# Hybrid decoder trunk on one Trainium2 core: order of the second layer's gates and retention outputs

## The chip, the core and the metric

The kernel runs on one core of one Trainium2 chip. The core has a matrix engine (PE, TensorE) that multiplies from SBUF into the eight banks of PSUM, a vector engine (DVE), an activation engine (ACT), GpSimd (POOL) and a queue (SP) that issues most transfers. Each engine works through its own list of instructions in order, and the lists are tied by semaphores. The metric is the time of one execution on the device in microseconds, lower is better.

## The reference

Two layers of a decoder trunk, over 512 tokens of width 1024, in f32. Of each layer:

```python
h = rmsnorm(x, g_mix)
z = h @ w_in
aq, ak, av, rq, rk, rv, rg, ga, gb = jnp.split(z, SPLIT_POINTS, axis=-1)
...
ya = sliding_window_sink_attention(aq, ak, av, sinks) @ w_a
...
r = chunkwise_retention(rq, rk, rv)
r = r * lax.rsqrt(jnp.mean(r * r, axis=-1, keepdims=True) + EPS)
r = r.reshape(B, S, RET_V) * jax.nn.silu(rg.astype(jnp.float32))
yb = r.astype(x.dtype) @ w_b
mixed = jax.nn.sigmoid(ga) * ya + jax.nn.sigmoid(gb) * yb
x = x + mixed @ w_out
h2 = rmsnorm(x, g_mlp)
x = x + jnp.square(jax.nn.relu(h2 @ w_up)) @ w_down
```

Retention has four heads, with 128 query and key columns and 256 value columns each. The change concerns the stretch from the values `rv` to the product with `w_b`: four heads of retention, their norm over 256 columns, the gated inputs `rg` (eight blocks of 128 columns, two for each head), and the gates `gb` (eight blocks).

## The kernel before

**Precision and tiles.** Activations are held transposed: 128 columns of the model on the partitions, 512 tokens along a row. Every operand of a large product is split into a high and a low part (`split`: ACT copies the high part as `r` or `hi`, DVE subtracts to get the low part as `r` or `lo`, L364/L365, L311/L312), and a product is three matmuls, high by high, high by low and low by high (`products`, L357 to L359). Weights come in units of 128x1024 (512 KB), loaded by SP into three `raw` buffers, split into three pairs of `hi` and `lo`, three units ahead of use. The list `unit_order` says in which order; it has to be the order of use.

**A chunk** (`chunk`) is one weight unit against all 512 tokens: 24 matmuls into one PSUM bank of `ps_mm` (five banks), after which a function evicts the bank. The chunks of `w_in` that matter here:

- `qk(h)`: k, then q of retention head h. `put_ret` rotates (`rotate`: two temps, `rot` and `rot2`, ACT L736/L737, DVE L740 to L742) and splits.
- `put_rg(i)`, i = 0..7: gated input i, scaled by the row norm into half of a `big` tile `z` (L1097), then Silu (L1104) for i >= 4 at once.
- `put_aside(c)`, c = 0..7: gate c into half of a `big` tile `gb` (L966), Sigmoid (L967), and for every second one a store to DRAM (`aside`), from which it is read back before its use.

**Values in the second layer** (`all_values`): seven block products (a Strassen-Winograd form, with the sums of the input made ahead), two weight units each, into `rv` banks. The first four value blocks `rv[0, n]` (heads 0 and 1) are complete after the fifth product, `rv[1, 2]` and `rv[1, 3]` (heads 2 and 3) after the sixth, `rv[1, 0]` and `rv[1, 1]` after the seventh. The bank pair `b` is read by DVE (`kept`, L1057) between the sixth and the seventh.

**Retention as a background.** `all_heads` is a generator whose steps are put between the parts of the chunks: each call `advance(rate)` adds the rate to a credit and takes one step for each whole unit of it. A chunk calls it twice, before each half of its matmuls; `all_values` 14 times with 0.6. A step emits instructions, so it sets the place of the work in the source. A head's steps: `scores` (two steps; products `ret`, tiles `s`, four in all), `outputs` (two steps; PSUM tiles `r` and `last` of `ps_aux`, three banks; `big` tile `rr`, temps `sq` and `rest`), `norm` (PSUM tile `ssq`, then square root and reciprocal into the temp `inv`), `finish` (products with `inv` and with `rr`, L1194/L1195, and a split for each half). After two heads `sum_heads` makes the sums that the block form of W_b needs (`sums`, L667 to L671, two `big` tiles), and splits them.

Three norms exist: `inverse_rms` (one square root and one reciprocal over 128x512), `inverse_rms_apart` (four square roots on 32 rows each, a reciprocal of 128x128, and a round trip through DRAM by two SP transfers, `row` and `inv`, L482/L483), and `inverse_rms_halved` (two square roots and a reciprocal over 256 columns, four copies back, L493 to L497). Heads 0 to 2 use the one that goes apart, head 3 `inverse_rms`. The MLP norm uses the halved one.

**Buffers.** `temp` tiles share one tag of six buffers of 128x512; `big` tiles one tag of seven of 128x1024.

**After the gates**: `drain` takes all steps that are left, then the first two pairs of W_b products (`mixed_pair`, `narrow_pair`: seven groups of 12 matmuls of 256 columns, the first pair in the three banks of `ps_aux`) read the splits of heads and sums.

**Order.** Engines don't follow the source strictly: the framework places each instruction on its engine's list by a simulation of the program, earlier source first among what is ready. What it has placed is fixed, and the chip then works through it.

The diff's places: `unit_order` (second layer's list), `Head.norm`, `Head.finish`, `all_heads`, and the calls at the end of the mix in `layer_body`. `Head` serves both layers, the rest of the edits the second alone.

Of the kernel before, what the change touches and what calls it, by code (L numbers as in the profile page):

```python
# [14 lines left out]
ALU = mybir.AluOpType  # L15
# [3 lines left out]
P = 128  # L19
T = 512  # L20
# [3 lines left out]
NB = T // P  # L24
# [5 lines left out]
RET_V = 256  # L30
# [29 lines left out]
def unit_order(last):  # L60

    def plain(name, *at):
        return [(name, i) for i in range(*at)]

    def pairs(src, *firsts):
        return [("pair", j, part, src) for j in firsts for part in range(4)]

    if last:
        order = plain("w_in", 22) + plain("w_a", 4)
        order += [("value", block, u) for block in range(len(VALUES)) for u in range(2)]  # L70
        order += plain("w_in", 26, 30) + plain("w_in", 34, 46)
    else:
        order = plain("w_in", 26) + plain("w_a", 4) + plain("w_in", 26, 46)
    order += pairs("w_b", 0, 2) + plain("w_b", 4, 8)
    order += plain("w_out", 2) + pairs("w_out", 2, 4, 6)
    for what, q, i in mlp_sequence():
        if what == "first":
            order += plain("w_up", 4)
        elif what == "pair":
            order += pairs("w_up", 8 * q + 2 * i)  # L80
        elif what == "down":
            order += plain("w_down", 8 * q + 2 * i, 8 * q + 2 * i + 2)
        else:
            order += plain("w_down", 8 * q, 8 * q + 8)
    return order


def mlp_sequence():

    seq = [("first", 0, 0), ("pair", 0, 2), ("pair", 0, 3)]
    for q in range(3):
        for i in range(4):
            seq += [("down", q, i), ("pair", q + 1, i)]
    return seq + [("last", 3, 0)]
# [32 lines left out]
def view(slot):  # L129
    return slot[0][:, slot[1], :]  # L130
# [3 lines left out]
def decoder(ctx, tc, xT, x_first, w_in, w_a, w_b, w_out, w_up, w_down, tables, decay, band, triangles, g_last, out):  # L134
    nc = tc.nc
# [10 lines left out]
    def f32(ap):  # L146
        return ap.bitcast(F32)
# [7 lines left out]
    def bank(pool, name):  # L155
        return pool.tile([P, T], F32, tag=pool.name, name=name)
# [15 lines left out]
    order = [(layer, *u) for layer in range(DEPTH) for u in unit_order(layer == DEPTH - 1)]  # L172
# [144 lines left out]
    def unit(name, layer):  # L317
        i = state["next"]
        assert order[i][:2] == (layer, name), (order[i], layer, name)
        state["next"] += 1  # L320
        split_until(i + 3)
        return parts.pop(i)
# [28 lines left out]
    def products(ps, pairs, start, stop, resume=False):  # L351


        n = len(pairs)
        for i, ((ah, al), (bh, bl)) in enumerate(pairs):
            more = {"skip_group_check": True} if resume else {}
            nc.tensor.matmul(ps, ah, bh, start=start and i == 0, stop=False, **more)  # L357
            nc.tensor.matmul(ps, ah, bl, start=False, stop=False, **more)  # L358
            nc.tensor.matmul(ps, al, bh, start=False, stop=stop and i == n - 1, **more)  # L359

    def split(hi, lo, src, scale=None):

        if scale is None:
            nc.scalar.activation(hi, src, AF.Copy)  # L364
            nc.vector.tensor_tensor(lo, src, f32(hi), ALU.subtract)  # L365
        else:
            nc.scalar.activation(hi, src, AF.Copy, scale=scale)
            nc.vector.scalar_tensor_tensor(lo, src, scale, f32(hi), ALU.mult, ALU.subtract)

    xs, x_homes = [], []  # L370
# [13 lines left out]
    def advance(rate=1.0):  # L384

        credit[0] += rate
        while credit[0] >= 1.0:
            credit[0] -= 1.0
            while background:
                try:  # L390
                    next(background[0])
                    break
                except StopIteration:
                    background.pop(0)
# [5 lines left out]
    def chunk(name, layer, moving, evacuate, rate=1.0):  # L400

        hi, lo = unit(name, layer)
        n = len(moving)
        ps = bank(ps_mm, "mm")
        pairs = [((hi[:, k * P : (k + 1) * P], lo[:, k * P : (k + 1) * P]), moving[k]) for k in range(n)]
        advance(rate)
        products(ps, pairs[: n // 2], True, False)
        advance(rate)
        products(ps, pairs[n // 2 :], False, True)
        evacuate(ps)  # L410
# [232 lines left out]
    def layer_body(layer):  # L643
        last_layer = layer == DEPTH - 1
# [351 lines left out]
        def qk(h, rate=1.0, between=lambda: None):  # L996
            chunk("w_in", layer, xs, put_ret(rk, h), rate)
            between()
            chunk("w_in", layer, xs, put_ret(rq, h), rate)

        rv = {}
# [86 lines left out]
        rg, rg_next, rg_tiles = {}, {}, {}  # L1088

        def put_rg(i):  # L1090
            def put(ps):
                if i % 2 == 0:
                    two = rg_tiles[i // 2] = big("z")
                    rg[i], rg_next[i + 1] = two[:, 0, :], two[:, 1, :]
                else:
                    rg[i] = rg_next.pop(i)
                nc.vector.tensor_tensor(rg[i], ps, rstd(), ALU.mult)  # L1097
                if i >= 4:
                    silu(i)

            return put
# [12 lines left out]
        class Head:  # L1114
# [70 lines left out]

            def norm(self):
                self.inv = temp("inv")
                (inverse_rms if self.h == 3 else inverse_rms_apart)(self.parts, RET_V, self.inv)

            def finish(self):  # L1190
                h = self.h
                for e in range(2):
                    z = rg.pop(2 * h + e)
                    nc.vector.tensor_tensor(z, z, self.inv, ALU.mult)  # L1194
                    nc.vector.tensor_tensor(z, self.rr[e], z, ALU.mult)  # L1195
                    hi, lo = slots.one(), slots.one()
                    split(view(hi), view(lo), z)
                    ret[2 * h + e] = (hi, lo)

        def retention(pair):  # L1200
# [34 lines left out]
        def all_heads():  # L1235
            four = [Head(h) for h in range(RET_HEADS)]

            def scores(h):
                while h not in rq:
                    yield  # L1240
                for js in ((0, 1), (2, 3)):
                    four[h].scores(js)
                    yield

            def outputs(h, *es):
                for e in es:
                    four[h].outputs(e)
                    yield

            yield from scores(0)  # L1250
            yield from scores(1)
            while (0, NB - 1) not in rv:
                yield
            yield from outputs(0, 0, 1)
            yield from outputs(1, 0)
            yield
            four[0].norm()
            yield
            yield from outputs(1, 1)
            yield from scores(2)  # L1260
            four[1].norm()
            yield
            yield from scores(3)
            for head in four[:2]:
                head.finish()
                yield
            sum_heads(0)
            yield
            yield from outputs(2, 0, 1)
            yield from outputs(3, 0)  # L1270
            four[2].norm()
            yield
            yield from outputs(3, 1)
            yield
            yield
            four[3].norm()
            yield
            for head in four[2:]:
                while 2 * head.h + 1 not in rg:
                    yield  # L1280
                head.finish()
                yield
            sum_heads(1)
# [27 lines left out]
        for u in range(4):  # L1311
            hi, lo = unit("w_a", layer)
            for j in range(2):
                c = 2 * u + j
# [15 lines left out]
        if last_layer:  # L1330
            background.append(all_heads())
            all_values(form_of(by_form_v), homes_v)
            qk(2, 1.1)
            qk(3, 1.1)
        else:
            background.append(retention(0))
            qk(2)
            qk(3)
            values(1)
            drain()  # L1340
            background.append(retention(1))
        for i in range(4, 8):
            chunk("w_in", layer, xs, put_rg(i), 1.1 if last_layer else 1.25)
        gates, gate_tiles, fresh = [], [], []

        def put_aside(c):
            def put(ps):
                if c % 2 == 0:
                    fresh[:] = [big("gb")]
                gate(fresh[0][:, c % 2, :])(ps)  # L1350
                if c % 2:
                    nc.sync.dma_start(aside[:, c - 1 : c + 1, :], fresh[0])

            return put

        for c in range(KD):
            chunk("w_in", layer, xs, put_aside(c), 1.1 if last_layer else 1.25)
        drain()
        old_input()

# [472 lines left out]
```

## Time and profile before

| | us |
|---|---|
| median of 3 runs | 1478.62 |
| lowest and highest | 1478.37, 1480.4 |
| profiled execution | 1478.1 |
| its span, first to last instruction | 1476.3 |

Times below are from the span's start. The second layer's values run to about 942, its qk chunks, gated inputs and gates from there to 1044.8, the W_b pairs from 1044.8. In the rows of the timeline stand the start, the duration, engine, line, operation, the tile written and the tiles read; in brackets the idle time of the engine before it and what ended it. In the list of waits stand the waiter, what it waited for, the total in us, how often and the longest. In the windows stand, for each engine, the busy time with the number of instructions, then the granted clock of PE (1.00 is full), the share of DMA and its rate. Matmul durations overlap, so their spacing is what counts.

### The profile page before, as it was taken

The numbers are of one execution on the slowest core, as the hardware profiler recorded it, in microseconds if no ns is written. First come the engines' busy times: TensorE is split into PE (matmuls) and PEld (weight loads), VectorE is DVE, ScalarE is ACT, GpSimd is POOL, SyncE is SP. The second block draws the span as 40 slices with busy tenths as digits, with TensorE's granted clock in tenths as the row PEclk, the third lists the DMA queues.
The fourth block names the chain that finished last, engine by engine and source line by source line (L and its number), as shares of the span: only waits on it lengthen the run. The fifth ranks groups of instructions, "written<-read, shape, count | busy, mean of one in ns | idle before, by whom it ended". The sixth has DMA issues, their size and how long they took to land.

```text
span 1476.3 us, 20312 instructions
## 1 busy us (share of the span) xinstructions
PE 1461.0 (99%) x7410; PEld 1245.2 (84%) x7410; DVE 1187.1 (80%) x1950; ACT 830.9 (56%) x1330; POOL 3.7 (0%) x14
## 2 busy tenths in 40 slices
PE   9999999999999999999999999999899999999998
PEld 7888888888988888888888888788789888888887
DVE  7998778678988787776898888677899877877774
ACT  7657356654784444544465675556547754455544
POOL 0000000000000000000000000000000000000000
PEclk9999999999999999999999999999899999999999
DMA  6423843356443333235963237633464432333363
GB/s 226 132 89 105 278 161 106 94 179 209 129 130 105 100 115 105 95 100 168 340 237 111 86 129 227 233 104 118 142 204 122 138 104 88 120 109 100 111 193 110
DMA packets 80548, 212.30 MB, mean 144 GB/s; under 512 B 9512, under 2 KB 9664, under 8 KB 80448
## 3 DMA queue, kind: packets, MB, share of 16 engines
q1 hardware_dynamic: 80160, 210.48, 44.5%
q8 instruction: 58, 0.95, 0.3%
q10 hardware_dynamic: 288, 0.52, 0.1%
q14 instruction: 42, 0.34, 0.1%
HBM read 183.16 MB, written 25.18 MB: 141 GB/s over the span
## 4 chain that ended last, share of the span: by engine, by line
PE 95%; DVE 2%; DMA 1%; issue 1%; ACT 0%; SPq 0%; POOLq 0%; DVEq 0%; ACTq 0%
PE mm L359 23%; PE mm L357 23%; PE mm L358 23%; PE mm L1517 11%; PE mm L1518 6%; PE rv L357 1%; PE rv L358 1%; PE rv L359 1%; PE score L905 1%; DMA park_w_out<-ahead 1%; DVE lo L312 1%; PE r L357 1%; PE r L359 0%; PE r L358 0%; PE pT L860 0%
## 5 line engine op out<-in xcount | busy, mean ns | idle before, releaser
L358 PE MATMUL mm<-r,hi 128*128 128x512 f32 (+1 forms) x1568 | 574.1, 368 | 2.6 <-DVE r L365 2.6
L357 PE MATMUL mm<-r,hi 128*128 128x512 f32 (+1 forms) x1568 | 571.0, 368 | 3.1 <-ACT r L364 2.8
L359 PE MATMUL mm<-r,lo 128*128 128x512 f32 (+1 forms) x1568 | 564.9, 368 | 0.3 <-DVE lo L312 0.2
L311 ACT ACTIVATE hi<-raw 128x1024 fp32r<-128x1024 f32 (+1 forms) x340 | 340.1, 1003 | 370.2 <-PE mm L358 200.6
L312 DVE TENSOR_TENSOR lo<-raw,hi 128x512 fp32r<-128x512 f32 (+1 forms) x341 | 391.7, 1151 | 106.5 <-ACT hi L311 105.2
L357 PEld LDWEIGHTS mm<-r,hi 128*128 128x128 f32 x1568 | 295.5, 189 | 50.7 <-ACT r L364 3.2
L358 PEld LDWEIGHTS mm<-r,hi 128*128 128x128 f32 x1568 | 295.9, 189 | 49.4 <-DVE r L365 3.2
L359 PEld LDWEIGHTS mm<-r,lo 128*128 128x128 f32 x1568 | 295.0, 189 | 48.8 <-DVE lo L312 1.5
L1517 PE MATMUL mm<-r,hi 128*128 128x512 f32 x728 | 251.9, 391 | 0.0
L1518 PE MATMUL mm<-r,lo 128*128 128x256 f32 x728 | 200.3, 277 | 0.0
L1517 PEld LDWEIGHTS mm<-r,hi 128*128 128x128 f32 x728 | 136.5, 188 | 28.8 <-ACT mm L1544 0.2
L1518 PEld LDWEIGHTS mm<-r,lo 128*128 128x128 f32 x728 | 136.7, 188 | 3.2 <-DVE lo L312 0.7
L1590 ACT ACTIVATE z<-z 128x512 f32<-128x512 f32 x56 | 32.4, 623 | 49.7 <-DVE z L1570 49.7
L1597 DVE TENSOR_TENSOR x<-x,mm 128x512 f32<-128x512 f32 x56 | 37.7, 685 | 24.1 <-PE mm L359 24.1
L364 ACT ACTIVATE r<-z 128x512 fp32r<-128x512 f32 x64 | 38.6, 620 | 16.5 <-DVE z L1195 16.4
L358 PE MATMUL rv<-lo,r 128*128 128x512 f32 x120 | 46.9, 390 | 0.4 <-DVE lo L312 0.4
L359 PE MATMUL rv<-hi,r 128*128 128x512 f32 x120 | 46.8, 390 | 0.0
L365 DVE TENSOR_TENSOR r<-z,r 128x512 fp32r<-128x512 f32 x64 | 42.9, 685 | 4.7 <-ACT r L364 4.3
L357 PE MATMUL rv<-hi,r 128*128 128x512 f32 x120 | 45.6, 392 | 0.9 <-DVE kept L1057 0.9
L932 ACT ACTIVATE sm<-sm,st 128x256 f32<-128x256 f32 (+1 forms) x64 | 30.1, 472 | 18.6 <-DVE st L920 18.6
L1570 DVE SCALAR_TENSOR_TENSOR z<-z,rstd 128x512 f32<-128x512 f32 x52 | 35.7, 686 | 0.6
L364 ACT ACTIVATE r<-sums 128x1024 fp32r<-128x1024 f32 x28 | 29.0, 1054 | 8.7 <-DVE sums L668 6.7
(281 smaller groups left out, 1708.9 us busy)
## 6 DMA issues: line engine op xcount, KB each, us to landing
raw<-w_in_in SPq DMA_DIRECT2D x87, 512.0 KB, 3.6
raw<-w_down_in SPq DMA_DIRECT2D x64, 512.0 KB, 3.6
raw<-w_up_in SPq DMA_DIRECT2D x32, 512.0 KB, 3.6
raw<-w_up_in SPq DMA_DIRECT2D x60, 256.0 KB, 2.9
raw<-w_a_in SPq DMA_DIRECT2D x8, 512.0 KB, 3.6
ahead<-w_b_in SPq DMA_DIRECT2D x8, 512.0 KB, 6.0
park_w_b<-ahead SPq DMA_DIRECT2D x16, 256.0 KB, 5.2
ahead<-w_up_in SPq DMA_DIRECT2D x8, 512.0 KB, 4.7
```

The lines of the kernel that those rows point to most:

```text
L311: nc.scalar.activation(hi[:, at], raw[:, at], AF.Copy)
L312: last_low[:] = [nc.vector.tensor_tensor(lo[:, at], raw[:, at], f32(hi[:, at]), ALU.subtract).ins]
L357: nc.tensor.matmul(ps, ah, bh, start=start and i == 0, stop=False, **more)
L358: nc.tensor.matmul(ps, ah, bl, start=False, stop=False, **more)
L359: nc.tensor.matmul(ps, al, bh, start=False, stop=stop and i == n - 1, **more)
L364: nc.scalar.activation(hi, src, AF.Copy)
L365: nc.vector.tensor_tensor(lo, src, f32(hi), ALU.subtract)
L1517: nc.tensor.matmul(both, hi[:, c], m, start=start and k == 0, stop=False, **more)
L1518: nc.tensor.matmul(ps[:, :H], lo[:, c], m[:, 0, :], start=False, stop=k == 3 and start, **more)
L1570: nc.vector.scalar_tensor_tensor(z[:, :, at], z[:, :, at], 0.0, factor, ALU.max, ALU.mult)
L1590: nc.scalar.activation(z[:, i, :], z[:, i, :], AF.Square)
L1597: nc.vector.tensor_tensor(x[:, c, :], x[:, c, :], ps, ALU.add)
```

## The change

Second layer only: the order of the chunks after the values, and with it the order of their weight units. Before: qk 2, qk 3, gated inputs 4 to 7, gates 0 to 7. After: qk 2, qk 3, gates 0 to 3, gated inputs 4 to 7, gates 4 to 7. The rate of the background in all of these goes from 1.1 to 1.25. The background waits for value block `(1, 1)` ahead of its first output, where it waited for `(0, 3)`.

Both layers: head 3's norm is the halved one, and `finish` multiplies the two halves of a head in one instruction each.

```diff
-        order += plain("w_in", 26, 30) + plain("w_in", 34, 46)
+        order += plain("w_in", 26, 30) + plain("w_in", 38, 42) + plain("w_in", 34, 38) + plain("w_in", 42, 46)
...
             def norm(self):
                 self.inv = temp("inv")
-                (inverse_rms if self.h == 3 else inverse_rms_apart)(self.parts, RET_V, self.inv)
+                (inverse_rms_halved if self.h == 3 else inverse_rms_apart)(self.parts, RET_V, self.inv)
 
             def finish(self):
                 h = self.h
+                two = rg_tiles[h]
+                nc.vector.tensor_tensor(two, two, self.inv.unsqueeze(1).broadcast_to([P, 2, T]), ALU.mult)
+                nc.vector.tensor_tensor(two, self.both, two, ALU.mult)
                 for e in range(2):
-                    z = rg.pop(2 * h + e)
-                    nc.vector.tensor_tensor(z, z, self.inv, ALU.mult)
-                    nc.vector.tensor_tensor(z, self.rr[e], z, ALU.mult)
                     hi, lo = slots.one(), slots.one()
-                    split(view(hi), view(lo), z)
+                    split(view(hi), view(lo), rg.pop(2 * h + e))
                     ret[2 * h + e] = (hi, lo)
...
-            while (0, NB - 1) not in rv:
+            while (1, 1) not in rv:
                 yield
...
-            qk(2, 1.1)
-            qk(3, 1.1)
+            qk(2, 1.25)
+            qk(3, 1.25)
...
-        for i in range(4, 8):
-            chunk("w_in", layer, xs, put_rg(i), 1.1 if last_layer else 1.25)
+        if not last_layer:
+            for i in range(4, 8):
+                chunk("w_in", layer, xs, put_rg(i), 1.25)
...
         for c in range(KD):
-            chunk("w_in", layer, xs, put_aside(c), 1.1 if last_layer else 1.25)
+            if last_layer and c == 4:
+                for i in range(4, 8):
+                    chunk("w_in", layer, xs, put_rg(i), 1.25)
+            chunk("w_in", layer, xs, put_aside(c), 1.25)
```

## The prediction

> **What bounds the kernel now.** I read the page first, for the busy shares; then the list of what TensorE (PE) waited for; then the windows and the timeline around the waits that the change touches.
>
> ```profile
> span 1476.3 us, 20312 instructions
> PE 1461.0 (99%) x7410; PEld 1245.2 (84%) x7410; DVE 1187.1 (80%) x1950; ACT 830.9 (56%) x1330; POOL 3.7 (0%) x14
> ```
> ```profile
> engine line waited for: us in total, times, longest us
> PE mm L357 <- ACT r L364: 2.8, 2, 1.4
> PE mm L358 <- DVE r L365: 2.6, 2, 1.7
> ...
> PE rv L357 <- DVE kept L1057: 0.9, 1, 0.9
> PE last L1166 <- ACT r L367: 0.6, 1, 0.6
> ...
> PE mm L359 <- DVE lo L312: 0.2, 1, 0.2
> PE last L1167 <- DVE r L368: 0.2, 1, 0.2
> ```
>
> PE is the bound, at 99%. The change neither adds nor removes a matmul, so it can only win back PE time that is lost, or lose more. The loss is in two places, both in the second layer: 5.4 us of waits of `mm` for `r` (2.8 + 2.6), and about 1.6 us around `rv` and `last` (0.9 + 0.6 + 0.2). In the first layer only the 0.2 us row of `lo` lies near work that the change touches. These rows show the larger place, at the first pair of W_b products:
>
> ```profile
> core 0: us, PE busy (x) PEld busy (x) DVE busy (x) ACT busy (x) POOL busy (x), PEclk, DMA share, GB/s
> 1044.70:1048.31 3.61, 3.61 (x31) 3.53 (x30) 3.61 (x4) 1.43 (x2) 0.00 (x0) 1.00 0.02 5
> 1048.31:1061.50 13.19, 7.77 (x33) 6.76 (x31) 11.49 (x17) 9.05 (x13) 0.00 (x0) 0.62 0.54 177
> ```
> ```profile
> 1049.91 0.39 PE L357 MATMUL mm<-r,hi 128*128 128x256 f32 x1 [1.43 <-ACT r L364]
> ...
> 1056.51 0.58 PE L358 MATMUL mm<-r,hi 128*128 128x256 f32 x1 [0.94 <-DVE r L365]
> ```
>
> Undisturbed, 31 products take 3.61 us, 0.1165 each. In the next 13.19 us only 33 are recorded, worth 3.84 us; three missing records would make it 4.2. So 9.0 to 9.35 us are lost there; **I take 9.2**. Of it 5.4 is waiting; the other 3.8 is the granted clock, 0.62 over the stretch.
>
> [...]
>
> What PE waits for is the end of the last retention head:
>
> ```profile
> 1042.24 0.69 ACT L504 ACTIVATE inv<-ssq,x 128x512 f32<-128x512 f32 x1 [2.11 <-PE ssq L503]
> 1042.96 3.35 DVE L505 RECIPROCAL inv<-inv 128x512 f32<-128x512 f32 x1 [1.58 <-ACT inv L504]
> 1047.31 1.28 DVE L1194 TENSOR_TENSOR z<-z,inv 128x512 f32<-128x512 f32 x2
> 1051.64 2.48 DVE L966 TENSOR_TENSOR gb<-mm,rstd 128x512 f32<-128x512 f32 x4
> 1056.70 1.22 DVE L365 TENSOR_TENSOR r<-sums,r 128x1024 fp32r<-128x1024 f32 x1
> ```
>
> Norm (1042.2 to 1046.3), products, sums and splits: 10.6 us from the first L1194 to the end of the last split, 1057.9, with four late gate evictions (2.5 us) in between. PE wanted it at 1048.3.
>
> **Why the head is late.** In the source its norm comes in the second gate chunk of eight, some 30 us earlier. The cause shows in when chunks are evicted. A weight split `hi` (L311) that waited for PE marks the end of a chunk; `rot` at L736 is the start of a q or k eviction.
>
> ```profile
> 949.35 1.06 ACT L311 ACTIVATE hi<-raw 128x1024 fp32r<-128x1024 f32 x1 [0.45 <-PE mm L358]
> 957.93 0.60 ACT L736 ACTIVATE rot<-mm 64x512 f32<-64x512 f32 x1
> 962.29 1.06 ACT L311 ACTIVATE hi<-raw 128x1024 fp32r<-128x1024 f32 x1 [2.50 <-PE mm L358]
> 967.73 1.06 ACT L311 ACTIVATE hi<-raw 128x1024 fp32r<-128x1024 f32 x1 [0.70 <-PE mm L358]
> ...
> 981.75 0.26 ACT L1141 ACTIVATE s<-ret 128x128 f32<-128x128 f32 x1
> 982.03 0.59 ACT L736 ACTIVATE rot<-mm 64x512 f32<-64x512 f32 x1
> ...
> 988.43 0.60 ACT L736 ACTIVATE rot<-mm 64x512 f32<-64x512 f32 x1
> ```
> ```profile
> 957.76 0.33 SPq L483 DMA_DIRECT2D inv<-row  x1
> ```
>
> A chunk takes 5.44 us (962.29 to 967.73). k of head 2 ended at 949.35 and was evicted at 957.93, right behind the issue of `inv` (957.76). k of head 3 ended at 962.29 and was evicted at 982.03, right behind the last `s` of head 2 (981.75). q of head 3 ended at 967.73, evicted at 988.43. All of these tiles share one tag of six buffers (`temp`), and each eviction starts just after the tile that precedes it in the source. I read this as: buffers of a tag are given out in source order, so the place of a background step decides which evictions stand behind it.
>
> **The change part by part.**
>
> Later outputs, rate 1.25. Nine background steps fit into the value product (14 calls at 0.6 on a credit of 0.8, left by two layers' 28 calls at 0.8, 22.4 each). Before, three of them were outputs, and in the qk chunks norm 0 stood ahead of k2, outputs(1,1) ahead of q2, all four `s` of head 2 ahead of k3. Now (0.2 + 1.25 a call): k2 stands ahead of outputs(1,0) and norm 0, q2 ahead of outputs(1,1), and only two `s` stand ahead of k3. So k2 can be evicted at its end (949.4, 8.5 us earlier), q2 some 6 us earlier, k3 once two `s` are made, about 968 (14 earlier). q3 still stands behind norm 1, which I put at about 978 (10 earlier). Scores of head 3, outputs of heads 2 and 3 and the last norm keep their mutual order (three PSUM banks) and follow by about 10 us: products at about 1037 instead of 1047.3, last split at about 1048. **The 9.2 us go.** Ends: nothing, if the delay is DVE's backlog instead, and 9.35.
>
> Outputs out of the value product. This is less than the words say, since the order on PE isn't the source's:
>
> ```profile
> 916.68 0.39 PE L357 MATMUL r<-r,r 128*128 128x512 f32 x1
> ...
> 931.89 0.28 PE L358 MATMUL r<-r,r 128*128 128x256 f32 x1
> 932.76 0.39 PE L1166 MATMUL last<-r,r 128*128 128x256 f32 x1 [0.59 <-ACT r L367]
> ...
> 936.27 0.50 PE L357 MATMUL rv<-hi,r 128*128 128x512 f32 x1 [0.88 <-DVE kept L1057]
> ```
>
> Output matmuls ran at 916.68, before the values that the source waits for existed: ready work is pulled into gaps. From 931.78 to 936.27 the value product itself is blocked by `kept`, and the outputs fill 2.9 of these 4.5 us. If they are still pulled in, nothing changes; if they are kept out, the two waits of `last` (0.75) go, or the 2.9 us of filler become idle. Ends −0.75 and +2.9; I take **0**, since the pulled row at 916.68 shows that readiness decides.
>
> Four gates ahead of the last four gated inputs. The same eight products and weight loads (512 KB each) in another order: 0 on PE. SP issues two `aside` stores earlier, between weight loads that themselves wait for PE; the most that can be held up behind them is a chunk, 5.4 us, covered by three units of prefetch. On ACT up to two more table loads, beside 44% idle. What it buys is room in the seven `big` buffers: these rows show the second pair of gated inputs held up:
>
> ```profile
> 973.40 0.69 DVE L1097 TENSOR_TENSOR z<-mm,rstd 128x512 f32<-128x512 f32 x1 [2.06 <-PE mm L359]
> 991.58 1.06 ACT L311 ACTIVATE hi<-raw 128x1024 fp32r<-128x1024 f32 x1 [1.95 <-PE mm L358]
> 1010.55 1.28 DVE L1097 TENSOR_TENSOR z<-mm,rstd 128x512 f32<-128x512 f32 x2
> ```
>
> The first input left PSUM at once; the last ended at 991.58 and left at 1010.55, 19 us on, behind the sums and outputs. A gate's buffer is freed by its store, a gated input's is held to the end. New cost: head 3 can't finish before the last gated input, which ends four chunks before W_b, at about 1044.8 − 4 × 5.44 = 1023; evicted at once, with table load and Silu, 1026, earlier than the 1037 above. Behind the new wait, on DVE and ACT, stand head 3's products, the second sums, their splits, and, since their buffers come after those of the sums, the evictions of gates 4 to 7; the first W_b pair waits for the splits. So 0, and the fifth rival if it isn't covered.
>
> Shorter norm, wider products:
>
> ```profile
> 1159.37 0.95 ACT L493 ACTIVATE own<-ssq,x 64x256 f32<-64x256 f32 x2 [2.31 <-PE ssq L489]
> 1162.14 1.70 ACT L497 ACTIVATE rstd<-own 64x256 f32<-64x256 f32 x4 [0.34 <-DVE own L494]
> ```
> ```profile
> L1408 DVE TENSOR_TENSOR gate<-gate,x x4: 1225/1226/1227, 330.9 to 1079.9; 128x1024 f32<-128x1024 f32 x4
> ```
>
> The halved norm, seen at the MLP norm, runs from 1159.37 to 1163.84, 4.5 us against 4.1 (1042.24 to 1046.31): its reciprocal is shorter, but copies come behind it. As a chain it is 0.4 us longer, though it frees DVE. Products: four of 0.6 us (two L1194 in 1.28) become two of 1.23 a head: no difference. Both edits also touch the first layer, where no PE wait stands behind them: 0, or 0.4 at worst.
>
> **Sum.** −9.2 + 0 + 0 + 0. The profiled execution took 1478.1 (span 1476.3 and 1.8 around it), 0.5 below the median of 1478.62. 1478.1 − 9.2 + 0.5 = **1469.4**.
>
> **The rivals.**
>
> 1. *Forecast*, 1467 to 1471: 0.50.
> 2. *Partly*: q3 is earlier by less than 8 us and one or two of the four waits stay. The last wait and the one before it (1.7 + 0.9) with half of the clock's 3.8 leave 4.5: 1473.9, within 1471 to 1475.6. For it: the margin that I find is nearly nil. 0.22.
> 3. *The filler is missing* in the value product: 2.9 us more idle, and a hole of 4.5 us in one piece; if the clock falls there as it did at W_b, 3.8 more: 1469.4 + 6.7 = 1476.1. Against it: the pulled rows. 0.05. [...]
> 4. *It doesn't do what it says*: the head is late because DVE is backed up, and the same work ends at the same time, with a norm that is 0.4 longer: 1479.0. For it: DVE's 80%; against it: evictions that start right behind one particular tile. 0.10.
> 5. *Slower*: the last gated input is the new gate. If it is evicted as late as before, head 3 finishes later than now. With 2.6 us for eviction, table load and Silu and 10.6 to the last split, it decides from an eviction 21.7 us after the chunk's end (1023 + 21.7 + 2.6 + 10.6 = 1057.9); every us beyond is one us lost. The two rows above show 19 us for the last input, and its neighbour, one chunk earlier, 24. At 24 to 30 us: 1481 to 1487, middle 1484. Against it: `big` is empty by then. 0.13.
>
> A measurement of this kernel tells about 0.2% (3 us) from no change. Faster by more (below 1475.7): 0.50 + 0.22 + 0.02 of the third = 0.74. Within: 0.03 + 0.10 = 0.13. Slower: 0.13. Range: 1467.0 to 1478.5 leaves out the slower case, half of the fourth and a little below, 0.2 together.
>
> **What would show it.** The q3 `rot` by 980 and the last norm before 1035; no wait of `mm` for `r` at the first W_b pair, and the granted clock at 1.00 there; the last `z` out of PSUM within 2 us of its chunk. A `rot` of q3 still near 988 speaks for the fourth, a late `z` for the fifth, a gap of 4 us before form 3 of the value product for the third. The forecast fails most easily by a new wait in this tight order.

## The result and the profile after

| | before | after |
|---|---|---|
| median, us | 1478.62 | 1472.68 |
| lowest and highest | 1478.37, 1480.4 | 1471.8, 1473.5 |
| runs | 5 | 5 |
| profiled execution, its span | 1478.1, 1476.3 | 1472.92, 1471.1 |

The ratio is 0.9957, with a 95% interval of 0.9943 to 0.9972: 5.9 us faster, where 9.2 were forecast. The time, 3.3 us above the predicted 1469.4, lies in the range but not in the forecast's own case (1467 to 1471): it is that of the second rival ("partly", 1471 to 1475.6).

The list of what PE waited for, from the second layer's values to the end of the first W_b pairs, in the changed kernel (waiter, releaser, total in us, times, longest):

```profile
PE mm L358 <- DVE r L365: 1.8, 2, 1.2
PE last L1166 <- ACT r L367: 1.0, 1, 1.0
PE rv L357 <- DVE kept L1057: 0.9, 1, 0.9
PE mm L357 <- ACT r L364: 0.8, 1, 0.8
PE rv L357 <- ACT hi L311: 0.6, 1, 0.6
PE rv L358 <- DVE lo L312: 0.5, 1, 0.5
PE mm L357 <- ACT eu L706: 0.3, 1, 0.3
PE last L1167 <- DVE r L368: 0.2, 1, 0.2
```

The waits of `mm` for `r` at W_b went from 5.4 us to 2.6 (1.8 + 0.8), with 0.3 for `eu` besides. Around `rv` and `last` the waits grew. What that means for the time is read from the windows: the value product and the first W_b pairs, first before, then after (busy time and instructions of PE, PEld, DVE, ACT and POOL, granted clock, DMA share and rate).

```profile
905.00:945.00 40.00, 37.95 (x176) 31.21 (x174) 32.03 (x48) 23.17 (x33) 0.00 (x0) 1.00 0.80 258
1045.00:1062.00 17.00, 11.58 (x64) 10.53 (x63) 14.99 (x21) 10.26 (x15) 0.00 (x0) 0.70 0.45 149
```
```profile
905.00:945.00 40.00, 36.86 (x166) 29.79 (x165) 31.18 (x47) 21.78 (x32) 0.00 (x0) 1.00 0.81 254
1045.00:1062.00 17.00, 14.09 (x106) 12.78 (x105) 15.20 (x21) 11.91 (x18) 0.00 (x0) 1.00 0.69 206
```

At W_b, the first W_b pairs, PE's idle time fell from 5.42 to 2.91 us: 2.5 won. The clock there went from 0.70 to 1.00: at 11.58 busy us, 11.58 × 0.30 = 3.5 more. In the value product the idle time grew from 2.05 to 3.14: 1.1 lost. That is 4.9 of the 5.2 us by which the span is shorter; 0.3 stay unassigned.

The timeline of the changed kernel shows how far the chain of the last head moved (start, duration, engine, line, operation). First the four rotations, the start of the evictions of k2, q2, k3 and q3:

```profile
950.01 0.59 ACT L736 ACTIVATE rot<-mm 64x512 f32<-64x512 f32 x1
959.02 0.60 ACT L736 ACTIVATE rot<-mm 64x512 f32<-64x512 f32 x1
969.70 0.60 ACT L736 ACTIVATE rot<-mm 64x512 f32<-64x512 f32 x1
983.39 0.60 ACT L736 ACTIVATE rot<-mm 64x512 f32<-64x512 f32 x1
```

Ahead of q3's rotation stands the issue of head 1's `inv`, as the prediction had it, but at 982.57 and not near 978:

```profile
982.57 0.33 SPq L483 DMA_DIRECT2D inv<-row  x1
```

Then the last gated input, head 3's first wide product, the four late gates and the last splits:

```profile
1021.81 0.69 DVE L1097 TENSOR_TENSOR z<-mm,rstd 128x512 f32<-128x512 f32 x1 [2.03 <-PE mm L359]
1043.57 1.23 DVE L1193 TENSOR_TENSOR z<-z,inv 128x1024 f32<-128x1024 f32 x1 [0.69 <-ACT inv L497]
1047.30 2.48 DVE L966 TENSOR_TENSOR gb<-mm,rstd 128x512 f32<-128x512 f32 x4
1052.63 2.36 DVE L365 TENSOR_TENSOR r<-sums,r 128x1024 fp32r<-128x1024 f32 x2
```

k2 left PSUM 7.9 us earlier than before, q2 5.0 and k3 12.3 earlier (forecast 8.5, 6 and 14), but q3 only 5.0 (forecast 10); head 3's product came 3.7 us earlier and the last split ended 2.9 earlier, at 1054.99. The last gated input was evicted as soon as PE had made it. The four late gate evictions still stand in the chain.

### The profile page after: what moved, and what is told of

Read it like the earlier page. It is cut to its first block, busy times and chain, and to the rows that moved or that the text cites. A ratio compares the mean times of both kernels' runs of the same rounds, so it can differ in the third digit from the quotient of the medians.

```text
span 1471.1 us, 20300 instructions
## 1 busy us (share of the span) xinstructions
PE 1458.1 (99%) x7410; PEld 1242.0 (84%) x7410; DVE 1183.5 (80%) x1934; ACT 831.9 (57%) x1338; POOL 3.7 (0%) x14
## 4 chain that ended last, share of the span: by engine, by line
PE 95%; DVE 2%; DMA 2%; issue 1%; ACT 0%; SPq 0%; POOLq 0%; DVEq 0%; ACTq 0%
PE mm L359 23%; PE mm L357 23%; PE mm L358 23%; PE mm L1521 11%; PE mm L1522 6%; PE rv L357 1%; PE rv L359 1%; PE rv L358 1%; DMA park_w_out<-ahead 1%; PE score L905 1%; DVE lo L312 1%; PE r L357 1%; PE r L359 1%; PE r L358 1%; PE pT L860 0%
## 5 line engine op out<-in xcount | busy, mean ns | idle before, releaser
L365 DVE TENSOR_TENSOR r<-sums,r 128x1024 fp32r<-128x1024 f32 x28 | 33.7, 1220 | 0.0
```

## The experiments

Twelve kernels ran, each several times and against the kernel before on the same chip, whose median was 1478.98, 1478.80 and 1479.80 in the three groups (1 to 4, 5 to 8, 9 to 12). The changed kernel's own median, 1472.68, was measured beside 1478.62, so a difference between it and a kernel of the third group can be off by about 1.2 us, in the others by 0.4 or less. Ratios stand with their 95% intervals. Line numbers are a few off where an edit adds lines.

**1. The order of the chunks undone.** The changed kernel with the gated inputs ahead of all gates, as before.

```diff
-        order += plain("w_in", 26, 30) + plain("w_in", 38, 42) + plain("w_in", 34, 38) + plain("w_in", 42, 46)
+        order += plain("w_in", 26, 30) + plain("w_in", 34, 46)
...
-        if not last_layer:
-            for i in range(4, 8):
-                chunk("w_in", layer, xs, put_rg(i), 1.25)
+        for i in range(4, 8):
+            chunk("w_in", layer, xs, put_rg(i), 1.25)
...
-            if last_layer and c == 4:
-                for i in range(4, 8):
-                    chunk("w_in", layer, xs, put_rg(i), 1.25)
```

> The changed kernel with one edit undone: the four gated inputs stand ahead of all gates again (weight order too); late outputs, rate 1.25, halved norm and wide products stay. Theory A (the place of the background steps in the source decides, through the shared temp buffers): the order of temps up to q of head 3 is unchanged, so that rotation stays near 983 us and the time near 1473. Theory B (room in the big tiles, which the new chunk order makes, is what brought the gain): the gated inputs take their big tiles ahead of the sums again, the head is late by 3 us or more, and the time goes back to 1476 to 1479.

Measured: 1476.31 (1475.14 to 1478.26, 11 runs), 0.9983 [0.9974, 0.9992]. The rotations are those of the changed kernel (982.97 for q3) and head 3's product comes at 1043.42, so the order doesn't make the chain earlier. It changes what stands around the chain's end. From the timelines, PE's waits and the end of its last gate chunk, then DVE's late evictions:

```profile
1046.62 0.58 PE L357 MATMUL mm<-r,hi 128*128 128x256 f32 x1 [2.88 <-ACT r L364]
1047.89 0.80 PE L357 MATMUL mm<-r,hi 128*128 128x512 f32 x1 [0.68 <-DVE gb L966]
...
1055.34 0.39 PE L359 MATMUL mm<-r,lo 128*128 128x512 f32 x1
...
1047.15 3.08 DVE L966 TENSOR_TENSOR gb<-mm,rstd 128x512 f32<-128x512 f32 x5
...
1055.76 0.69 DVE L966 TENSOR_TENSOR gb<-mm,rstd 128x512 f32<-128x512 f32 x1 [1.47 <-PE mm L359]
```

Five gate evictions stand in a row instead of four, as many as `ps_mm` has banks. The chunk of the eighth gate, 24 matmuls from 1047.89 to 1055.7, stands behind the first W_b products in PE's list and waits for a bank (0.68). So PE asks for head 3's split at 1043.74, 4.2 us earlier than in the changed kernel (1047.93), and waits 2.88 us for a chain that isn't late, while a whole chunk lies behind the wait. That the full banks put the chunk there is my reading; its place is in the rows. PE was idle for 3.85 us, and the clock fell. The prediction had priced this edit at 0; without it most of the 5.9 us are gone.

**2. The late wait undone.** The changed kernel with the background waiting for `(0, NB - 1)` again.

```diff
-            while (1, 1) not in rv:
+            while (0, NB - 1) not in rv:
```

> The changed kernel with one edit undone: the background waits for value block (0,3) again, so three outputs come into the value product's steps; everything else stays. Theory A: norm 0 stands ahead of k of head 2 again and all four s ahead of k of head 3; rotation of q of head 3 near 988, time 1476 to 1479. Theory B: the time stays within 1.5 us of 1472.7.

Measured: 1475.61 (1475.31 to 1477.55, 11 runs), 0.9981 [0.9973, 0.9990], 0.4 us below the range of theory A. The four rotations start at 959.52, 965.62, 983.62 and 990.02: all back to where they stood before (957.93, 964.03, 982.03, 988.43), 1.6 us later even, though the rate is 1.25. One condition in the generator, which adds no instruction, moves the eviction of k2 by 9.5 us and that of k3 by 13.9. This is the prediction's mechanism: the place of a step in the source decides which evictions stand behind it.

**3. The halved norm undone.** The changed kernel with `inverse_rms` for head 3.

```diff
-                (inverse_rms_halved if self.h == 3 else inverse_rms_apart)(self.parts, RET_V, self.inv)
+                (inverse_rms if self.h == 3 else inverse_rms_apart)(self.parts, RET_V, self.inv)
```

> The changed kernel with the last head's norm as before (one square root and one reciprocal over 512 columns, no copies). By the rows its chain is 4.1 us against 4.5, so the first product of head 3 comes 0.4 us earlier and the time is 1472.3, within 1 us of the changed kernel. Rival (the shorter reciprocal is what counts, since DVE is the one that is behind): 1.6 us more on DVE, 1474 or more.

Measured: 1476.15 (1473.17 to 1477.09, 11 runs), 0.9980 [0.9971, 0.9989]: the rival's time, not the 1472.3 of the rows. Head 3's product comes 1.0 us later than in the changed kernel, not 0.4 earlier; 0.4 of it lies ahead of the norm (`ssq` at 1039.07 against 1038.63), 0.6 is the longer norm. That product, PE's waits at W_b, and the clock in windows of 2 us there:

```profile
1044.57 1.21 DVE L1193 TENSOR_TENSOR z<-z,inv 128x1024 f32<-128x1024 f32 x1
...
1048.55 0.38 PE L357 MATMUL mm<-r,hi 128*128 128x256 f32 x1 [0.17 <-ACT mm L703]
1052.69 0.44 PE L358 MATMUL mm<-r,hi 128*128 128x256 f32 x1 [1.99 <-DVE r L365]
1055.03 0.58 PE L358 MATMUL mm<-r,hi 128*128 128x256 f32 x1 [0.94 <-DVE r L365]
```
```profile
1054.00:1056.00 2.00, 1.06 (x5) 0.97 (x5) 2.00 (x3) 0.93 (x1) 0.00 (x0) 0.50 1.00 403
1056.00:1058.00 2.00, 2.00 (x11) 1.95 (x10) 1.14 (x2) 1.49 (x3) 0.00 (x0) 0.50 0.02 6
```

PE is busy all through 1056 to 1058, at half clock, with 11 matmuls recorded; the changed kernel has 20 in the same window. The waits are 3.1 us against 2.9, and yet the kernel is 3.5 us slower. The price isn't in the waiting but in the clock, which fell behind one wait of 1.99 us in place of three of 0.80, 1.19 and 0.63.

**4. A buffer of its own for `inv`.** The changed kernel, where the second layer's `inv` leaves the tag `temp` for the tag `rstd`, which has two buffers. One of them is in use there (the gates are scaled by `rstd`), the other idle.

```diff
-                self.inv = temp("inv")
+                if last_layer:
+                    self.inv = tmp.tile([P, T], F32, tag="rstd", name="inv", bufs=2)
+                else:
+                    self.inv = temp("inv")
```

> The changed kernel with the second layer's inv tiles taken from the idle buffer of the rstd tag instead of temp. Nothing is computed otherwise. Theory A: q of head 3 no longer stands behind the norm of head 1, its rotation starts by 977 instead of 983, the first product of head 3 by 1040, the waits at the first W_b pair fall from 2.9 to under 1.5 us, time 1469 to 1471. Rival (DVE's backlog sets the end, whatever the buffers): no move, 1472.7.

Measured: **1468.70** (1467.79 to 1468.76, 5 runs), 0.9930 [0.9916, 0.9944], the fastest of all kernels here. q3's rotation and the last splits in the timeline, and the window at W_b:

```profile
976.12 0.59 ACT L736 ACTIVATE rot<-mm 64x512 f32<-64x512 f32 x1
...
1040.14 2.38 DVE L365 TENSOR_TENSOR r<-sums,r 128x1024 fp32r<-128x1024 f32 x2
```
```profile
1045.00:1062.00 17.00, 17.00 (x147) 17.00 (x146) 11.60 (x16) 10.09 (x16) 0.00 (x0) 1.00 0.79 253
```

The edit removes no work; it takes one tile out of a tag of six. q3 is evicted 7.3 us earlier, the last split ends at 1042.52, 12.5 earlier, and PE has no wait at W_b. So the shared tag is what still held the chain in the changed kernel.

**5. The second sums behind all gates.** In the changed kernel `sum_heads(1)` waits until all eight gate chunks are out, to clear the four late evictions out of the chain.

```diff
+            while len(done_gates) < KD:
+                yield
             sum_heads(1)
...
             chunk("w_in", layer, xs, put_aside(c), 1.25)
+            done_gates.append(c)
```

> The changed kernel; the second sums of heads 2 and 3 are emitted only when all eight gates stand in the source, so the last four gates get their big tiles ahead of the sums. Theory (source order of big tiles): the four late gate evictions (2.5 us on DVE) leave the last chain, which ends 2.5 us earlier, and the waits at the first W_b pair fall from 2.9 to about 0.5 us: 1470 to 1471. Rival (those evictions fill time in which DVE would wait anyway): no move, 1472.7.

Measured: 1473.15 (1472.67 to 1474.12, 5 runs), 0.9962 [0.9949, 0.9975]: nothing gained. The evictions came earlier, three of them ahead of head 3's products (1029.87, 1037.01 and 1040.98) and one between these (1046.98); the first product started at 1045.84, 2.3 us later. PE's idle time at W_b is 2.90 us, as in the changed kernel. DVE's work in this stretch only changed places.

**6. The rate of before.** The changed kernel with 1.1 in place of 1.25 for qk, gated inputs and gates.

```diff
-            qk(2, 1.25)
-            qk(3, 1.25)
+            qk(2, 1.1)
+            qk(3, 1.1)
...
-                    chunk("w_in", layer, xs, put_rg(i), 1.25)
-            chunk("w_in", layer, xs, put_aside(c), 1.25)
+                    chunk("w_in", layer, xs, put_rg(i), 1.1)
+            chunk("w_in", layer, xs, put_aside(c), 1.1 if last_layer else 1.25)
```

> The changed kernel with one edit undone: the background's rate in the chunks after the values is 1.1 again. By the count of steps norm 0 and outputs(1,1) move one call later and the end of the head two calls; q of head 3 stands behind the same tiles but for two s, so its rotation stays within 2 us of 983. Theory A: the last chain ends within 1 us of the changed kernel's, but every us there costs a wait and near 3 us of waits the clock falls: 1473 to 1477. Rival (the rate is what brings the gain): 1478 or more.

Measured: 1469.46 (1468.15 to 1469.70, 5 runs), 0.9935 [0.9922, 0.9948]. Neither side had this: the slower rate is faster by 3.2 us. q3's rotation stayed within 2 us of 983, as expected, but the chain ended 4.0 us earlier (1050.97), not within 1. Rotations and head 3's product:

```profile
956.59 0.60 ACT L736 ACTIVATE rot<-mm 64x512 f32<-64x512 f32 x1
964.98 0.60 ACT L736 ACTIVATE rot<-mm 64x512 f32<-64x512 f32 x1
981.32 0.60 ACT L736 ACTIVATE rot<-mm 64x512 f32<-64x512 f32 x1
...
1038.42 1.22 DVE L1193 TENSOR_TENSOR z<-z,inv 128x1024 f32<-128x1024 f32 x1 [0.69 <-ACT inv L497]
```

q2 leaves 2.4 us earlier than at 1.25, k3 4.7 earlier, and head 3's product comes 5.2 earlier. I read it as the same mechanism with its sign turned: counted by the credit, fewer steps are in the source ahead of each eviction. The change's wait helps, its rate hurts.

**7. The buffer for `inv` alone.** The kernel before with the edit of experiment 4 and nothing of the change.

> The kernel before, with only the second layer's inv tiles taken from the idle buffer of the rstd tag. Theory A: k of head 2 and q of head 3 no longer wait for the norms' inv, so q of head 3 is rotated about 6 us earlier than 988.4; all four s of head 2 still stand ahead of k of head 3. The head ends some 4 us earlier, waits at W_b fall from 5.4 to 2 or less, the clock stays: 1470 to 1473. Rival (the place of outputs and gates in the change is needed): 1476 or more.

Measured: 1474.54 (1472.67 to 1477.03, 10 runs), 0.9972 [0.9962, 0.9981], between theory and rival. q3's rotation and the window at W_b:

```profile
984.42 0.60 ACT L736 ACTIVATE rot<-mm 64x512 f32<-64x512 f32 x1
```
```profile
1045.00:1062.00 17.00, 13.70 (x92) 12.43 (x91) 14.23 (x22) 11.06 (x17) 0.00 (x0) 0.90 0.65 211
```

q3's rotation comes 4.0 us earlier than before, where 6 were expected; head 3's product, at 1043.93, 3.4 earlier; PE is idle for 3.30 us at W_b, not 2 or less, at a clock of 0.90. One buffer in the old kernel is worth some 4.3 us, against 5.9 for the whole change.

**8. Outputs kept out of the value product.** In the changed kernel the second layer's output matmuls are tied behind the last matmul of the value product, which is what the change's words say. `last_mm` holds the last matmul that `products` emitted.

```diff
...
+            value_end[:] = last_mm
...
-                    four[h].outputs(e)
+                    with tc.issue_after(value_end[0]):
+                        four[h].outputs(e)
```

> The changed kernel with the output matmuls of the second layer tied behind the last matmul of the value product, so that they really stay out of it. The row-based price: the gap in which DVE reads bank b is no longer filled, 2.9 us more idle there in one piece of 4 to 5 us; if the clock falls, up to 3.8 more: 1475.5 to 1479.5. Rival (the outputs in the value product only add waits): 1471 to 1472.

Measured: 1478.07 (1476.19 to 1481.56, 11 runs), 0.9997 [0.9988, 1.0006]. PE's waits in the value product:

```profile
929.06 0.73 PE L357 MATMUL rv<-hi,r 128*128 128x512 f32 x2 [1.85 <-ACT hi L311]
930.32 0.50 PE L358 MATMUL rv<-lo,r 128*128 128x512 f32 x1 [0.53 <-DVE lo L312]
935.87 0.47 PE L357 MATMUL rv<-hi,r 128*128 128x512 f32 x1 [1.51 <-DVE kept L1057]
```

The gaps that outputs had filled become waits of 3.89 us instead of 3.14, with a clock of 0.96 over 905 to 945: 0.75 and 1.4 us lost there. As much is lost at W_b, where the chain is late again (q3's rotation at 989.12): 3.49 us idle at a clock of 0.90, 0.6 and 1.4 us more than in the changed kernel. The time lies in the expected range, but not by its sum: the idle time of the value product grew by 0.75 us and not by 2.9, with no hole of 4 to 5 us (the longest gap is 1.85), and half of the loss came at W_b. Still, in the changed kernel the outputs are no hindrance to the value product but a filler of it; in the kernel before that wasn't tried.

**9. The late wait alone.** The kernel before with the edit of experiment 2 turned round.

> The kernel before with one edit of the change: the background waits for value block (1, 1) ahead of its first output. Rate 1.1, order of chunks, norm and products as before. Theory (the source place of background steps decides): the four rotations start as in the changed kernel with rate 1.1, near 950, 957, 965 and 981, the first product of head 3 near 1039 to 1042, at most 2 us of waits for r at W_b, clock above 0.9 there; 1470 to 1473. Rival (the parts only work together: with the gated inputs ahead of the gates the chain is cut by late evictions as where that order was undone): one wait near 3 us at W_b and the clock near half speed, 1476.

Measured: 1477.01 (1476.15 to 1478.38, 11 runs), 0.9983 [0.9975, 0.9992]: the rival's time. Its one wait near 3 us came as three (0.69, 2.27 and 0.94), with a clock of 0.80. Rotations, and head 3's product, in this kernel:

```profile
951.16 0.60 ACT L736 ACTIVATE rot<-mm 64x512 f32<-64x512 f32 x1
957.89 0.60 ACT L736 ACTIVATE rot<-mm 64x512 f32<-64x512 f32 x1
966.27 0.60 ACT L736 ACTIVATE rot<-mm 64x512 f32<-64x512 f32 x1
983.81 0.60 ACT L736 ACTIVATE rot<-mm 64x512 f32<-64x512 f32 x1
...
1045.97 1.28 DVE L1194 TENSOR_TENSOR z<-z,inv 128x512 f32<-128x512 f32 x2
```

The rotations moved as the theory says, by 4.6 to 15.8 us, but head 3's product by only 1.3. An early rotation isn't an early head.

**10. The halved norm and the wide products alone.** The kernel before with these two edits and nothing else.

> The kernel before with the halved norm for head 3 and the wide products alone. Theory (my prediction's price: the chain is 0.4 us longer and nothing else moves; waits and a low clock at W_b stay): 1478.5 to 1479.5, first product near 1047.5. Rival (the halved norm is worth as much by itself as it cost to undo, because it frees DVE): 1475 to 1476.

Measured: 1476.41 (1475.26 to 1477.92, 11 runs), 0.9977 [0.9969, 0.9986]: the rival again, not the theory. Head 3's product is at 1046.71, 0.6 us earlier, and PE's idle time at W_b is 3.81 us against 5.42, at a clock of 0.71. The profiled run (1477.92) is the slowest of the eleven, so its trace doesn't show where 3.4 us come from; the size stands, its place stays open.

**11. Rate 1.1 and the buffer for `inv` together.** The edits of experiments 4 and 6.

> The changed kernel with both edits that helped alone: rate 1.1, and the second layer's inv in its own buffers. Theory (both remove the same 2.9 us of waits at W_b, the buffer all of them): no more than with the buffer alone, 1468.4 to 1469.0. Rival (the rate also removes gaps elsewhere): 1466 to 1467.5.

Measured: 1469.43 (1468.13 to 1471.02, 5 runs), 0.9931 [0.9917, 0.9945]. No more than either alone, as the theory said: of the 2.91 us of waits at W_b the rate leaves 0.85, the buffer none, both together 0.30.

**12. The buffer, and the sums of the values later.** Experiment 4, with `sum_ahead` of the last value forms put behind the reading of bank pair `b`.

```diff
-            sum_ahead()
...
+            sum_ahead()
```

> The changed kernel with the second layer's inv in its own buffers, and in the second layer's values the sums made ahead are put in the source behind the reading of bank pair b instead of ahead of it. Theory (the wait of the last value product for kept is DVE being busy with these sums): that wait of 0.9 us goes, 1467.8 to 1468.2. Rival (kept itself, behind the sixth product, is what takes the time, or its place on DVE is chosen by readiness): the wait stays, 1468.5 to 1469.

Measured: 1469.72 (1468.51 to 1470.49, 5 runs), 0.9934 [0.9921, 0.9946]. What PE waited for:

```profile
PE rv L358 <- DVE lo L312: 1.3, 2, 0.8
PE mm L357 <- ACT mm L703: 0.7, 1, 0.7
PE mm L357 <- ACT eu L706: 0.3, 1, 0.3
PE rv L357 <- ACT hi L311: 0.2, 1, 0.2
```

The wait for `kept` is gone, and the idle time of the value product fell from 2.69 to 1.49 us; the theory on that wait was right. The time didn't fall: 1.04 us of waits came at W_b, where experiment 4 has none. With the 1.20 won before, that would leave the span 0.2 shorter; it is 0.9 longer, so 1.1 us were lost in neither place, and where isn't known.

**All kernels in one table.** "Values" is PE's idle time from 905 to 945, "W_b" that from 1045 to 1062 (in experiment 1 with the 1.26 us that lie ahead of 1045), "clock" the granted clock of that second window, all from the one profiled execution of each kernel, "lost to it" PE's busy time there times (1 − clock). The last column is the span less values, W_b and lost.

| kernel | span | values | W_b | clock | lost to it | rest |
|---|---|---|---|---|---|---|
| before | 1476.3 | 2.05 | 5.42 | 0.70 | 3.5 | 1465.4 |
| 10 norm, products alone | 1476.1 | 2.94 | 3.81 | 0.71 | 3.8 | 1465.5 |
| 9 late wait alone | 1475.9 | 3.20 | 3.89 | 0.80 | 2.6 | 1466.2 |
| 2 late wait undone | 1475.7 | 3.97 | 4.26 | 0.80 | 2.5 | 1464.9 |
| 8 outputs kept out | 1474.8 | 3.89 | 3.49 | 0.90 | 1.4 + 1.4 (values) | 1464.6 |
| 1 order undone | 1473.7 | 3.13 | 3.85 | 0.80 | 2.9 | 1463.8 |
| 3 norm undone | 1473.7 | 3.65 | 3.11 | 0.80 | 2.8 | 1464.2 |
| 7 buffer alone | 1472.8 | 3.42 | 3.30 | 0.90 | 1.4 | 1464.7 |
| 5 sums last | 1471.3 | 2.85 | 2.90 | 1.00 | 0 | 1465.6 |
| after | 1471.1 | 3.14 | 2.91 | 1.00 | 0 | 1465.1 |
| 11 rate and buffer | 1469.2 | 3.92 | 0.30 | 1.00 | 0 | 1465.0 |
| 6 rate 1.1 | 1467.8 | 3.17 | 0.85 | 1.00 | 0 | 1463.8 |
| 12 buffer, sums later | 1466.7 | 1.49 | 1.04 | 1.00 | 0 | 1464.2 |
| 4 buffer | 1465.8 | 2.69 | 0 | 1.00 | 0 | 1463.1 |

The spans differ by 10.5 us, what is left without the three losses by 3.1. So most of what these edits do to the time is done in two short stretches. Each row is one execution, and the values' idle time also differs where no edit touches the value product (2.05 before, 2.94 in 10, 3.42 in 7), so differences of about 1 us in that column don't tell edits apart.

## Why the prediction was right, and where it was off

**The place of the loss: right.** The prediction put 9.2 us at the first W_b pairs, part waits, part clock. The kernel of experiment 4 has neither there, and is 10.3 us faster than before on the same chip (1478.98 to 1468.70). The share of the clock, 3.8, is borne out: it is 3.5 by the window of 17 us and 3.7 by windows of 0.1 us, and the changed kernel won it whole, though 2.9 us of waits remain there at clock 1.00. Short gaps went with a fall of the clock elsewhere too: in experiment 3 it fell to 0.50 with no gap above 1.99 us.

**The mechanism: right.** That the place of a background step in the source decides which evictions stand behind it, through the buffers of the shared tag, is shown by experiment 2 (a condition moves four evictions) and by experiment 4 (one tile fewer in the tag); experiment 6 (fewer steps ahead) fits it.

**The step that failed** is "Scores of head 3, outputs of heads 2 and 3 and the last norm keep their mutual order … and follow by about 10 us". Two sizes in it were wrong. q3 was put at 978, 10 us earlier; it came at 983.39, 5 earlier, behind head 1's `inv` as forecast, but that `inv` came 4.6 us later than forecast (982.57). And a shift at the rotation isn't handed on whole. Starts from the timelines, with the end of the last split in the last column:

| kernel | q3 `rot` | `s` of head 3 | norm 2 `ssq` | norm 3 `ssq` | product of head 3 | splits end |
|---|---|---|---|---|---|---|
| before | 988.43 | 1004.75 | 1025.0 | 1041.8 | 1047.31 | 1057.92 |
| 9 late wait alone | 983.81 | 1001.84 | 1025.0 | 1040.5 | 1045.97 | 1057.58 |
| after | 983.39 | 997.14 | 1023.4 | 1038.6 | 1043.57 | 1054.99 |
| 6 rate 1.1 | 981.32 | 995.85 | 1018.1 | 1033.5 | 1038.42 | 1050.97 |
| 4 buffer | 976.12 | 990.10 | 1011.5 | 1025.8 | 1032.27 | 1042.52 |

In the changed kernel a lead of 7.6 us at the first `s` of head 3 is 1.6 at norm 2. Of the 6 us, 2.7 are gone within head 3's scores: from its first `s` to its last (L1141) it takes 6.2 us (997.14 to 1003.34), 3.5 before (1004.75 to 1008.20). Behind the scores lie the outputs of head 2. ACT's timeline of the changed kernel shows one thing that now falls into this stretch:

```profile
1012.01 0.63 ACT L1175 ACTIVATE sq<-rr 128x512 f32<-128x512 f32 x1 [0.74 <-DVE rr L1173]
1012.71 0.60 ACT L1171 ACTIVATE rr<-r 128x512 f32<-128x512 f32 x1
1013.32 1.28 ACT L1104 ACT_TABLE_LOAD   x1
1014.62 1.15 ACT L1104 ACTIVATE z<-z 128x512 f32<-128x512 f32 x2
1015.79 0.63 ACT L463 ACTIVATE rest<-sq 64x512 f32<-64x512 f32 x1
```

Table load and Silu of the gated inputs stand between head 2's `sq` and its `rest`, 2.4 us. There `rest` starts 2.8 us after the sum of the squares (L1183, 1013.03); before and in experiment 6, where they don't stand between, 0.7 us after it (1016.93 to 1017.65, 1008.27 to 1009.00). I take this for 2 of the 6 us; no run here tried it by itself. It isn't the new order that does it: in experiment 1 a table load and two Sigmoids of the gates stand in the same place (1012.91 to 1015.36). What stretches the scores, and the last 1.3 us, stay open.

**Outputs out of the value product: 0.** The value product's idle time grew by 1.1 us, within the ends of −0.75 and +2.9, but no run shows that this edit did it: with the wait undone (2) the idle time is 3.97, not less than 3.14. The reason given was right: outputs still run ahead of their source place, and experiment 8 shows what happens if they don't. Which transfers or splits make the waits for `hi` and `last` longer wasn't tried.

**Gates ahead of the gated inputs: 0 was wrong.** The order alone, undone, costs 3.6 us (1476.31 against 1472.68). The prediction saw the room in the `big` buffers, but followed it to the gated inputs only. It missed PE's list at W_b: with five gates waiting for eviction instead of four, the last gate's chunk stood behind the first W_b products (experiment 1).

**Norm and products: 0 was wrong.** Undone, the halved norm costs 3.5 us; alone, with the wide products, it gains 3.4. Its chain isn't 0.4 us longer, as forecast, but no longer or shorter: from `ssq` to product it takes 4.9 us in the changed kernel (1038.63 to 1043.57) against 5.5 in experiment 3, and 5.5 in experiment 10 as before. The rest of the 3.5 is the clock, which fell in experiment 3 (2.8 us). The wide products weren't tried alone.

**The rate: wrong sign.** Taken as a part of the shift, it takes 3.2 us of it back.

**The signs.** Of those named in advance, q3's rotation by 980, the last norm before 1035 and no wait of `mm` for `r` didn't come (983.39, 1038.6, 2.6 us); the clock at 1.00 and the last `z` out at once did. That the time still lay in the range is in part luck: terms put at nothing, or booked with the wrong sign, were worth about 3 us each, and partly cancelled.

**The rivals.** The fifth (a late last gated input) didn't occur: it was evicted at 1021.81, right behind PE. The third had no hole (the longest gap in the changed kernel's value product is 1.01 us). The fourth (DVE backed up) is refuted by experiment 4, in which DVE has the same work. The second is what happened, not quite as worded: the four waits for `r` became three shorter ones, and none of the clock's 3.8 us stayed, where half was put.

The parts don't add up: undone one by one, order, wait and norm cost 3.6, 2.9 and 3.5 us, and the rate −3.2, 6.8 together against 5.9. I read this so: each takes away some of the same margin at W_b, and the clock's price didn't grow with the idle time: with order, wait and norm undone the clock is 0.80 each time, at 3.85, 4.26 and 3.11 us of it.

## What to carry to other kernels

Where work in the background shares a tag of buffers with the evictions of the main path, count which tiles of the tag stand ahead of each eviction in the source; here one tile moved to a tag with an idle buffer was worth 4.3 us alone, and 4.0 on top of the change's 5.9. A lead at the start of a chain is worth only what is left of it at the wait that ends last, so follow it through each engine before it is booked. Before an edit is priced at nothing because its chain is as long as the old one, look at the waits behind it and at the granted clock there: with the norm undone, 3.1 us of waits in place of 2.9 came with a clock of 0.80 in place of 1.00 and a time 3.5 us longer.

## What the hardware showed

In the profiled executions, the granted clock at W_b stayed at 1.00 with up to 2.91 us of idle time in the 17 us (after, 5, 6, 11, 12, 4); from 3.11 us on (3, 7, 8, 10, 1, 9, 2, before) it shows 0.70 to 0.90. That isn't a limit on the sum: in experiment 3 it fell at about 1052.9, behind only 2.16 us of idle time (0.17 and 1.99). Nor is it the longest gap: in experiment 10 it fell at about 1052.2, where no gap ahead of the fall was above 1.1 us, while the changed kernel kept the clock with one of 1.19 and experiment 5 with one of 1.23.

The trace of the kernel before, in windows of 0.02 us, shows two values of the clock there: 1.00, and 0.50 from 1051.44 to 1061.67, 10.2 of the 17 us. In experiment 3, by the windows of 2 us, it is 0.50 from about 1052.9 to 1059.7, and from 1055.03 on PE is busy without a gap, so 4.7 us of that lie behind the waits: the price came in part after them. In experiment 8 the clock falls in the value product too (0.91 over 925 to 945): from 931.16 the rows of PE stand 0.43 us apart in place of 0.23, behind gaps of 1.85 and 0.53. What decides when the clock falls and when it comes back isn't shown by these runs.

The clock also differs between runs of one kernel: experiment 7's went from 1472.67 to 1477.03 us, with mean clocks from 0.996 to 1.000, and experiment 5's mean clock is 1.000 in the profiled run and 0.998 in the other four.
